# Two chained matrix products on one core: opening with half rows of a, slices of b behind each half

## Chip, cores, metric

One core of a Trainium2 chip. The metric is the device time of the whole kernel in microseconds (us), as the median of several runs. Ratios are the mean time of one kernel's fast runs over that of the kernel before in the same rounds, so they are not quite the ratio of the medians quoted.

## The reference

```python
m, k, n, p = 1024, 1024, 2048, 1024
h = np.matmul(a, b)
h = 0.5 * h * (1 + np.tanh(np.sqrt(2 / np.pi) * (h + 0.044715 * h ** 3)))   # gelu
return np.matmul(h, c).astype(np.float32)
```

## The kernel before

The change touches the first quarter of the kernel. There h11, the first quadrant of h, is made from the first 512 rows of a and the first 1024 columns of b. Block mt of a is 128 rows; slice k of b is 128 rows by 1024 columns (512 KB in float32). Each block is cast to bfloat16 in two halves, each half is turned on TensorE by four 128x128 transposes into PSUM and copied into aT. Each slice is cast and then taken by tiles t (128 columns of b, one PSUM bank each).

```python
for mt in R:                    # R = range(4)
    load_a0(mt, 1)              # whole rows: 128 x 1024 float32, one load
for k in range(KT):             # KT = 8
    load_b0(k, 1)
...
warm_up(8)                      # matmuls without use, that raise the clock
...
for mt in range(3):
    cast_a0(mt, 0)              # left half on VectorE
    cast_a0(mt, 1)              # right half on ScalarE
    pt = [turn0(mt, 0), turn0(mt, 1)]
    ...
    copy0(mt, 0, pt[0])
    copy0(mt, 1, pt[1])
    warm_up((3, 6, 2)[mt])
...
for k in range(1, KT):
    if k + 1 < KT:
        cast_b0(k + 1)
    for t in range(N0 + 1 if k < 4 else N0):    # N0 = 6
        mm0(t, (k,))
```

Later, when the second half of a is turned (the four "turns" on the line of `turn`), tile 6 catches up on four slices and tile 7 on seven. After that nothing differs between the two kernels.

Of the kernel before, what the change touches and what calls it, by code (L numbers as in the profile page):

```python
# [9 lines left out]
F32 = mybir.dt.float32  # L10
BF16 = mybir.dt.bfloat16
# [3 lines left out]
AF = mybir.ActivationFunctionType  # L15
# [4 lines left out]
def kernel(ctx, tc, a, b, c, out):  # L20
    nc = tc.nc
    M, K = a.shape
    _, N = b.shape
    _, P = c.shape
    KT = K // 128
    NT = N // 128
    MT = M // 128
    H = 512
    N0 = 6
    W0 = N // 2  # L30
    KH = KT // 2
    NH = NT // 2
    R = range(4)

    av = a.rearrange("(mt p) k -> p mt k", p=128)
    bv = b.rearrange("(kt p) n -> p kt n", p=128)
# [5 lines left out]
    astage = ctx.enter_context(tc.tile_pool(name="astage", bufs=4))  # L42
    abf = ctx.enter_context(tc.tile_pool(name="abf", bufs=4))
    b0stage = ctx.enter_context(tc.tile_pool(name="b0stage", bufs=6))
    opool = ctx.enter_context(tc.tile_pool(name="opool", bufs=4))
    ppool = ctx.enter_context(tc.tile_pool(name="ppool", bufs=6, space=PSUM))
    tpool = ctx.enter_context(tc.tile_pool(name="tpool", bufs=2, space=PSUM))

    warm = consts.tile([128, H], BF16, name="warm")
# [11 lines left out]
                               for g in range(2)] for h in range(2)]  # L61


    a_st, b_st = {}, {}

    def load_a0(mt, parts):
        st = astage.tile([128, K], F32, name="a_st")
        w = K // parts
        for i in range(parts):
            nc.sync.dma_start(out=st[:, ts(i, w)], in_=av[:, mt, ts(i, w)])  # L70
        a_st[mt] = st

    def load_b0(k, parts):
        st = b0stage.tile([128, W0], F32, name="b0_st")
        w = W0 // parts
        for i in range(parts):
            nc.sync.dma_start(out=st[:, ts(i, w)], in_=bv[:, k, ts(i, w)])
        b_st[k] = st

    gate = consts.tile([128, 1], F32, name="gate")  # L80
    for mt in R:
        load_a0(mt, 1)
    for k in range(KT):
        load_b0(k, 1)

    nc.gpsimd.tensor_copy(gate, b_st[4][:, 0:1])
    g = consts.tile([128, 1], F32, name="g")
    nc.scalar.activation(g, warm[:, 0:1], AF.Gelu_apprx_tanh)

    side = [ppool.tile([128, 8, 128], BF16, name="ps", tag="ps") for _ in range(2)]  # L90
    ps = [ppool.tile([128, H], F32, name="ps", tag="ps") for _ in range(4)]

    def warm_up(n):
        for _ in range(n):
            nc.tensor.matmul(ps[3], warm[:, 0:128], warm, start=True, stop=True)  # L95

    warm_up(8)
    ab = []

    def cast_a0(mt, g):  # L100
        if g == 0:
            ab.append(abf.tile([128, K], BF16, name="ab1"))
            nc.vector.tensor_copy(ab[mt][:, 0:512], a_st[mt][:, 0:512])
        else:
            nc.scalar.activation(ab[mt][:, 512:K], a_st[mt][:, 512:K], AF.Copy)  # L105

    def turn0(mt, g):
        if mt == 2:
            pt = side[g]
        elif (mt, g) == (3, 1):  # L110
            pt = ps[5][:, :].bitcast(BF16).rearrange("p (k m) -> p k m", k=8)
        else:
            pt = tpool.tile([128, 8, 128], BF16, name="pt", tag="pt")
        for k in range(4):
            nc.tensor.transpose(pt[:, k, :], ab[mt][:, ts(4 * g + k, 128)], ident)  # L115
        return pt

    def copy0(mt, g, pt):
        dst = aT[0][:, ts(g, 4), ts(mt, 128)]
        if g == 0 or mt == 3:  # L120
            nc.vector.tensor_copy(dst, pt[:, 0:4, :])  # L121
        else:
            nc.scalar.activation(dst, pt[:, 0:4, :], AF.Copy)  # L123

    HW = W0 // 2

    def cast_b0(k):
        v = {0: ((HW, W0),), 1: ((0, 256), (256, HW))}.get(k, ((0, HW),))
        a = {0: ((0, 256), (256, HW))}.get(k, ((HW, W0),))
        for i in range(max(len(v), len(a))):  # L130
            if i < len(a):
                nc.scalar.activation(b_lo[:, k, slice(*a[i])], b_st[k][:, slice(*a[i])], AF.Copy)  # L132
            if i < len(v):
                nc.vector.tensor_copy(b_lo[:, k, slice(*v[i])], b_st[k][:, slice(*v[i])])  # L134

    for mt in range(3):
        cast_a0(mt, 0)
        cast_a0(mt, 1)
        pt = [turn0(mt, 0), turn0(mt, 1)]
        if mt == 2:  # L140
            cast_a0(3, 0)
        copy0(mt, 0, pt[0])
        copy0(mt, 1, pt[1])
        warm_up((3, 6, 2)[mt])
    copy0(3, 0, turn0(3, 0))
    warm_up(2)
    ps += [ppool.tile([128, H], F32, name="ps", tag="ps") for _ in range(2)]
    cast_b0(0)
    cast_a0(3, 1)

    def mm0(t, ks):
        for k in ks:
            nc.tensor.matmul(ps[t], b_lo[:, k, ts(t, 128)], aT[0][:, k, :],  # L153
                             start=(k == 0), stop=(k == KT - 1))

    late = [tpool.tile([128, H], F32, name="pt", tag="pt") for _ in range(2)]
    ps += late[::-1]
    for t in R:
        mm0(t, (0,))
    copy0(3, 1, turn0(3, 1))  # L160
    for t in (4, 7, 6, 5):
        mm0(t, (0,))
    cast_b0(1)
    for k in range(1, KT):
        if k + 1 < KT:
            cast_b0(k + 1)
        for t in range(N0 + 1 if k < 4 else N0):
            mm0(t, (k,))

    def gelu(dst, src):  # L170
        nc.scalar.activation(dst, src, AF.Gelu_apprx_tanh)  # L171

    def bank(w=H):
        return ppool.tile([128, w], F32, name="ps", tag="ps", padded_shape=[128, H])
# [6 lines left out]
    for j in R:  # L181
        st = abf.tile([128, K], BF16, name="ab1")
# [7 lines left out]
    def turn(j):  # L190
        pt = ppool.tile([128, KT, 128], BF16, name="ps", tag="ps")
        for k in range(KT):
            nc.tensor.transpose(pt[:, k, :], a1[j][:, ts(k, 128)], ident)  # L193
        nc.vector.tensor_copy(aT[1][:, :, ts(j, 128)], pt)
        nc.scalar.activation(a22[:, :, ts(j, 128)], aT[1][:, KH:KT, ts(j, 128)], AF.Copy)
# [12 lines left out]
                             start=(k == 0), stop=(k == KT - 1))  # L208
        gelu(dst, p)

    mm0(6, range(4, KT))
    gelu(h11[:, 6, :], ps[6])
    mm0(7, range(1, 4))
    turn(0)
    turn(1)
    mm0(7, range(4, KT))
    turn(2)
    gelu(h11[:, 7, :], ps[7])
    mm1_half(0, 0)
# [80 lines left out]
    for j in R:  # L300
        p = bank()
        prod(p, KH, whole(bx), whole(aT[0]), j)
        nc.scalar.activation(v2[:, j, :], p, AF.Copy)
    for j in R:
        p = bank()
# [4 lines left out]
    for j in R:  # L310
        p = bank()
# [8 lines left out]
    for j in R:  # L320
        p = bank()
# [10 lines left out]
    for j in R:  # L332
        p = bank()
# [5 lines left out]
    for j in R:  # L339
        p = bank()  # L340
# [24 lines left out]
    for j in R:  # L365
        p = bank()
# [29 lines left out]
    for j in R:  # L396
        p = bank()
# [4 lines left out]
    for j in R:  # L402
        p = bank()
# [5 lines left out]
    for j in R:  # L409
        p = bank()  # L410
# [8 lines left out]
    for j in R:  # L419
        p = bank()  # L420
# [3 lines left out]
    for j in R:  # L424
        p = bank()
        prod(p, NH, halves(s2), whole(c22), j)
        combine(j, 1, p, p5[:, j, :])
    for j in R:
        p = bank()
        prod(p, NH, whole(h22), pairs(t2), j)  # L430
        combine(4 + j, 0, p, u3[j])
    for j in range(3):
        p = bank()
        prod(p, NH, whole(h12), whole(c21), j)
        combine(j, 0, p, p1[:, j, :])
    for q0, w, queue in ((0, 256, nc.sync), (256, 128, nc.scalar), (384, 128, nc.sync)):
        p = bank(w)
# [33 lines left out]
```

## Time and profile before

| | before |
|---|---|
| median, lowest, highest of the first 3 runs | 120.69, 120.44, 120.73 us |
| span of the profiled run | 118.3 us |
| TensorE busy | 113.4 us, 96% |
| first useful matmul | 10.10 us |
| end of the third turn of the second half of a | 25.67 us |
| landing of b slices 0, 1, 4, 7 | 9.54, 11.63, 15.49, 19.31 us |

The landings are when the last of the 16 increments of a load's semaphore is recorded in the trace.

### The profile page before, as it was taken

The numbers are of one execution on the slowest core, as the hardware profiler recorded it, in microseconds if no ns is written. First come the engines' busy times: TensorE is split into PE (matmuls) and PEld (weight loads), VectorE is DVE, ScalarE is ACT, GpSimd is POOL, SyncE is SP. The second block draws the span as 40 slices with busy tenths as digits, with TensorE's granted clock in tenths as the row PEclk, the third lists the DMA queues.
The fourth block names the chain that finished last, engine by engine and source line by source line (L and its number), as shares of the span: only waits on it lengthen the run. The fifth ranks groups of instructions, "written<-read, shape, count | busy, mean of one in ns | idle before, by whom it ended". The sixth has DMA issues, their size and how long they took to land.

```text
span 118.3 us, 1597 instructions
## 1 busy us (share of the span) xinstructions
PE 113.4 (96%) x583; PEld 76.1 (64%) x589; DVE 82.3 (70%) x113; ACT 45.7 (39%) x77; POOL 26.6 (22%) x39
## 2 busy tenths in 40 slices
PE   5999999999999999999999999999999999999990
PEld 2454444589744445888887447888888888886460
DVE  0355422068999908999999999995789992824450
ACT  5366544978342565206469998330000000000000
POOL 2000069752200000095205329000006500000000
PEclk9999999999999999999999999999999999999999
DMA  3999999999999999959999999999997999944434
GB/s 115 385 395 302 421 418 227 188 368 378 212 209 206 207 205 378 350 137 244 255 229 204 190 195 198 180 206 141 151 159 171 245 266 350 342 184 152 177 118 148
DMA packets 13543, 28.41 MB, mean 240 GB/s; under 512 B 992, under 2 KB 5472, under 8 KB 13536
## 3 DMA queue, kind: packets, MB, share of 16 engines
q0 software_dynamic: 9216, 17.83, 73.0%
q1 hardware_dynamic: 4176, 10.42, 23.6%
q8 instruction: 4, 0.07, 0.2%
q10 hardware_dynamic: 144, 0.07, 0.2%
q14 instruction: 3, 0.02, 0.1%
HBM read 20.97 MB, written 4.19 MB: 213 GB/s over the span
## 4 chain that ended last, share of the span: by engine, by line
PE 95%; ACT 1%; DVE 1%; issue 1%
PE ps L269 64%; PE ps L153 9%; PE ps L207 7%; PE ps L95 4%; PE ps L200 4%; PE pt L153 3%; PE ps L193 2%; PE pt L115 1%; PE ps L115 1%; ACT aT L123 1%; ACT ab L105 0%; DVE aT L121 0%; DVE ot L440 0%; DVE warm L50 0%
## 5 line engine op out<-in xcount | busy, mean ns | idle before, releaser
L269 PE MATMUL ps<-t,s 128*128 128x512 f32 x64 | 14.9, 392 | 0.0
L269 PE MATMUL ps<-c,h 128*128 128x512 bf16 (+2 forms) x78 | 14.1, 336 | 0.1
L269 PEld LDWEIGHTS ps<-t,s 128*128 128x128 f32 x64 | 12.0, 188 | 2.6
L277 DVE TENSOR_TENSOR ot<-ps,v 128x512 f32<-128x512 f32 x16 | 10.4, 681 | 3.2 <-PE ps L269 3.2
L269 PE MATMUL ps<-t,h 128*128 128x512 f32 x48 | 11.7, 389 | 0.0
L171 ACT ACTIVATE h<-ot 128x512 bf16<-128x512 f32 (+1 forms) x16 | 9.4, 622 | 5.9 <-DVE ot L277 5.9
L269 PEld LDWEIGHTS <-h 128*128 128x128 bf16 x80 | 7.1, 98 | 7.0 <-issue 0.5
L171 ACT ACTIVATE h<-ps 128x512 bf16<-128x512 f32 (+2 forms) x17 | 8.3, 526 | 8.4 <-PE ps L207 5.9
L153 PE MATMUL ps<-aT,b_lo 128*128 128x512 bf16 x46 | 11.2, 379 | 0.2
L385 DVE TENSOR_TENSOR ot<-ps,p 128x512 f32<-128x512 f32 x11 | 7.5, 688 | 5.5 <-PE ps L269 3.1
L153 PEld LDWEIGHTS <-b_lo 128*128 128x128 bf16 x64 | 6.1, 98 | 7.5 <-DVE b_lo L134 0.5
L269 PEld LDWEIGHTS ps<-t,h 128*128 128x128 f32 x48 | 9.0, 188 | 1.9
L207 PE MATMUL ps<-aT,b_lo 128*128 128x512 bf16 x39 | 8.7, 379 | 0.1
L95 PE MATMUL ps<-warm 128*128 128x512 bf16 x21 | 7.1, 475 | 1.2 <-DVE warm L50 1.2
L269 PE MATMUL ps<-as,bt 128*128 128x512 f32 x32 | 7.6, 396 | 0.0
L287 POOL DMA_DIRECT2D c<-in_c_dram x8 | 6.3, 833 | 5.6 <-DMA b<-in_b_dram 3.9
L269 PE MATMUL ps<-as,b 128*128 128x512 f32 x32 | 7.4, 389 | 0.0
L269 PE MATMUL ps<-c,s 128*128 128x512 f32 x32 | 7.4, 389 | 0.0
L269 PE MATMUL ps<-aT,bx 128*128 128x512 bf16 x31 | 7.0, 379 | 0.1
L418 POOL DMA_DIRECT2D t<-c x4 | 3.5, 1042 | 15.5 <-PE ps L269 14.4
L132 ACT ACTIVATE b_lo<-b_st 128x512 bf16<-128x512 f32 (+1 forms) x9 | 5.1, 581 | 4.8 <-DMA b_st<-in_b_dram 4.8
L134 DVE CAST b_lo<-b_st 128x512 bf16<-128x512 f32 (+1 forms) x9 | 3.5, 394 | 5.0 <-DMA b_st<-in_b_dram 5.0
(71 smaller groups left out, 172.0 us busy)
## 6 DMA issues: line engine op xcount, KB each, us to landing
b_st<-in_b_dram SPq DMA_DIRECT2D x8, 512.0 KB, 8.9
out_dram<-ot SPq DMA_DIRECT2D x15, 256.0 KB, 2.1
c<-in_c_dram POOLq DMA_DIRECT2D x6, 512.0 KB, 17.8
t<-c POOLq DMA_DIRECT2D x6, 512.0 KB, 6.6
a_st<-in_a_dram SPq DMA_DIRECT2D x4, 512.0 KB, 4.8
b<-in_b_dram POOLq DMA_DIRECT2D x2, 1024.0 KB, 10.3
c<-in_c_dram POOLq DMA_DIRECT2D x2, 1024.0 KB, 20.7
t<-t POOLq DMA_DIRECT2D x4, 512.0 KB, 8.6
```

The lines of the kernel that those rows point to most:

```text
L95: nc.tensor.matmul(ps[3], warm[:, 0:128], warm, start=True, stop=True)
L132: nc.scalar.activation(b_lo[:, k, slice(*a[i])], b_st[k][:, slice(*a[i])], AF.Copy)
L134: nc.vector.tensor_copy(b_lo[:, k, slice(*v[i])], b_st[k][:, slice(*v[i])])
L153: nc.tensor.matmul(ps[t], b_lo[:, k, ts(t, 128)], aT[0][:, k, :], start=(k == 0), stop=(k == KT - 1))
L171: nc.scalar.activation(dst, src, AF.Gelu_apprx_tanh)
L200: nc.tensor.matmul(p, b_lo[:, k, ts(t, 128)], aT[1][:, k, ts(q, 256)], start=(k == 0), stop=(k == KT - 1))
L207: nc.tensor.matmul(p, b_lo[:, k, ts(t, 128)], aT[h][:, k, :], start=(k == 0), stop=(k == KT - 1))
L269: nc.tensor.matmul(p, lhs(t)[:, ts(j, 128)], rhs(t)[:, q], start=(t == 0), stop=(t == n - 1))
L277: tt(ot, p, u, op=ADD)
L287: nc.gpsimd.dma_start(out=dst[:, t:t + 4, :], in_=cv[:, r * NH + t:r * NH + t + 4, ts(q, H)])
L385: tt(ot, p, u, op=ADD)
L418: nc.gpsimd.dma_start(out=t2[i], in_=c21[:, P2[i], :], accum_op=ADD)
```

## The change

Its intent is to have useful matmuls sooner. With the left half rows of a alone, four of the eight slices of b can be used. So 1 MB of a comes first, then four slices, then the right half rows, then four slices. Seven tiles take every slice, in place of seven and then six. The turns need PSUM while seven tiles are open: the first turns use banks of tiles that have not begun, the second ones the bank of tile 7, one half of it for even blocks and one for odd.

```diff
-    for mt in R:
-        load_a0(mt, 1)
-    for k in range(KT):
-        load_b0(k, 1)
+    for g in range(2):
+        load_a0(g)               # four loads: 128 x 512 each
+        for k in range(g * KH, g * KH + KH):
+            load_b0(k)
 ... (cut)
+    def turned(mt, g):
+        if g == 0:
+            return ps[mt][:, :].bitcast(BF16)[:, 0:512].rearrange("p (k m) -> p k m", k=4)
+        return ps[7][:, :].bitcast(BF16)[:, ts(mt % 2, 512)].rearrange("p (k m) -> p k m", k=4)
 ... (cut: four left halves are cast, turned and copied, with 10 warm-ups between)
+    for k in range(KH):
+        if k + 1 < KH:
+            cast_b0(k + 1)
+        else:
+            cast_a0(0, 1, True)
+            cast_a0(1, 1, False)
+        for t in range(7):
+            mm0(t, (k,))
+            if k + 1 == KH and t == 3:
+                turn0(0, 1)
+                copy0(0, 1, True)          # True: VectorE, False: ScalarE
+    turn0(1, 1)
+    copy0(1, 1, False)
+    cast_a0(2, 1, True)
+    turn0(2, 1)
+    cast_a0(3, 1, True)
+    copy0(2, 1, False)
+    turn0(3, 1)
+    copy0(3, 1, True)
+    for k in range(KH, KT):
+        cast_b0(k)
+        for t in range(7):
             mm0(t, (k,))
 ... (cut)
-    mm0(6, range(4, KT))
     gelu(h11[:, 6, :], ps[6])
-    mm0(7, range(1, 4))
+    mm0(7, range(KH))
     turn(0)
     turn(1)
-    mm0(7, range(4, KT))
+    mm0(7, range(KH, KT))
```

More of the change, by code (lines that the diff above doesn't have):

```diff
@@ L61, with load_a0, load_b0 @@
                                for g in range(2)] for h in range(2)]
-    a_st, b_st = {}, {}
-    def load_a0(mt, parts):
-        st = astage.tile([128, K], F32, name="a_st")
-        w = K // parts
-        for i in range(parts):
-            nc.sync.dma_start(out=st[:, ts(i, w)], in_=av[:, mt, ts(i, w)])
-        a_st[mt] = st
-    def load_b0(k, parts):
-        st = b0stage.tile([128, W0], F32, name="b0_st")
-        w = W0 // parts
-        for i in range(parts):
-            nc.sync.dma_start(out=st[:, ts(i, w)], in_=bv[:, k, ts(i, w)])
-        b_st[k] = st
+    a_st = [astage.tile([128, K], F32, name="a_st") for _ in R]
+    b_st = {}
+    def load_a0(g):
+        for mt in R:
+            nc.sync.dma_start(out=a_st[mt][:, ts(g, H)], in_=av[:, mt, ts(g, H)])
+    def load_b0(k):
+        b_st[k] = b0stage.tile([128, W0], F32, name="b0_st")
+        nc.sync.dma_start(out=b_st[k], in_=bv[:, k, 0:W0])
     gate = consts.tile([128, 1], F32, name="gate")
-    for mt in R:
-        load_a0(mt, 1)
-    for k in range(KT):
-        load_b0(k, 1)
+    for g in range(2):
+        load_a0(g)
+        for k in range(g * KH, g * KH + KH):
+            load_b0(k)
     nc.gpsimd.tensor_copy(gate, b_st[4][:, 0:1])
@@ L88, with cast_a0, copy0 @@
     nc.scalar.activation(g, warm[:, 0:1], AF.Gelu_apprx_tanh)
-    side = [ppool.tile([128, 8, 128], BF16, name="ps", tag="ps") for _ in range(2)]
-    ps = [ppool.tile([128, H], F32, name="ps", tag="ps") for _ in range(4)]
+    ps = [ppool.tile([128, H], F32, name="ps", tag="ps") for _ in range(N0)]
+    ps += [tpool.tile([128, H], F32, name="pt", tag="pt") for _ in range(2)]
     def warm_up(n):
         for _ in range(n):
-            nc.tensor.matmul(ps[3], warm[:, 0:128], warm, start=True, stop=True)
+            nc.tensor.matmul(ps[5], warm[:, 0:128], warm, start=True, stop=True)
     warm_up(8)
-    ab = []
-    def cast_a0(mt, g):
+    ab = [abf.tile([128, K], BF16, name="ab1") for _ in R]
+    def turned(mt, g):
         if g == 0:
-            ab.append(abf.tile([128, K], BF16, name="ab1"))
-            nc.vector.tensor_copy(ab[mt][:, 0:512], a_st[mt][:, 0:512])
+            return ps[mt][:, :].bitcast(BF16)[:, 0:512].rearrange("p (k m) -> p k m", k=4)
+        return ps[7][:, :].bitcast(BF16)[:, ts(mt % 2, 512)].rearrange("p (k m) -> p k m", k=4)
+    def cast_a0(mt, g, vector):
+        if vector:
+            nc.vector.tensor_copy(ab[mt][:, ts(g, H)], a_st[mt][:, ts(g, H)])
         else:
-            nc.scalar.activation(ab[mt][:, 512:K], a_st[mt][:, 512:K], AF.Copy)
+            nc.scalar.activation(ab[mt][:, ts(g, H)], a_st[mt][:, ts(g, H)], AF.Copy)
     def turn0(mt, g):
-        if mt == 2:
-            pt = side[g]
-        elif (mt, g) == (3, 1):
-            pt = ps[5][:, :].bitcast(BF16).rearrange("p (k m) -> p k m", k=8)
-        else:
-            pt = tpool.tile([128, 8, 128], BF16, name="pt", tag="pt")
+        pt = turned(mt, g)
         for k in range(4):
             nc.tensor.transpose(pt[:, k, :], ab[mt][:, ts(4 * g + k, 128)], ident)
-        return pt
-    def copy0(mt, g, pt):
+    def copy0(mt, g, vector):
         dst = aT[0][:, ts(g, 4), ts(mt, 128)]
-        if g == 0 or mt == 3:
-            nc.vector.tensor_copy(dst, pt[:, 0:4, :])
+        if vector:
+            nc.vector.tensor_copy(dst, turned(mt, g))
         else:
-            nc.scalar.activation(dst, pt[:, 0:4, :], AF.Copy)
+            nc.scalar.activation(dst, turned(mt, g), AF.Copy)
     HW = W0 // 2
@@ L134, in cast_b0 @@
                 nc.vector.tensor_copy(b_lo[:, k, slice(*v[i])], b_st[k][:, slice(*v[i])])
-    for mt in range(3):
-        cast_a0(mt, 0)
-        cast_a0(mt, 1)
-        pt = [turn0(mt, 0), turn0(mt, 1)]
-        if mt == 2:
-            cast_a0(3, 0)
-        copy0(mt, 0, pt[0])
-        copy0(mt, 1, pt[1])
-        warm_up((3, 6, 2)[mt])
-    copy0(3, 0, turn0(3, 0))
-    warm_up(2)
-    ps += [ppool.tile([128, H], F32, name="ps", tag="ps") for _ in range(2)]
+    cast_a0(0, 0, True)
+    turn0(0, 0)
+    warm_up(2)
+    cast_a0(1, 0, False)
+    copy0(0, 0, True)
+    turn0(1, 0)
+    warm_up(2)
+    cast_a0(2, 0, True)
+    copy0(1, 0, False)
+    turn0(2, 0)
+    warm_up(2)
+    cast_a0(3, 0, True)
+    copy0(2, 0, False)
+    turn0(3, 0)
+    warm_up(4)
+    copy0(3, 0, True)
     cast_b0(0)
-    cast_a0(3, 1)
     def mm0(t, ks):
@@ L154, in mm0 @@
                              start=(k == 0), stop=(k == KT - 1))
-    late = [tpool.tile([128, H], F32, name="pt", tag="pt") for _ in range(2)]
-    ps += late[::-1]
-    for t in R:
-        mm0(t, (0,))
-    copy0(3, 1, turn0(3, 1))
-    for t in (4, 7, 6, 5):
-        mm0(t, (0,))
-    cast_b0(1)
-    for k in range(1, KT):
-        if k + 1 < KT:
-            cast_b0(k + 1)
-        for t in range(N0 + 1 if k < 4 else N0):
+    for k in range(KH):
+        if k + 1 < KH:
+            cast_b0(k + 1)
+        else:
[17 more added lines that the diff above has]
+        for t in range(7):
             mm0(t, (k,))
```

## The prediction

> **What bounds the kernel now.** I read the page first (busy rows, then the chain that ended last), then the chain in order of time, then the timeline and one-microsecond windows of the first 31 us, where the whole change lies.
>
> The page's busy rows and chain:
>
> ```profile
> PE 113.4 (96%) x583; PEld 76.1 (64%) x589; DVE 82.3 (70%) x113; ACT 45.7 (39%) x77; POOL 26.6 (22%) x39
> ...
> PE 95%; ACT 1%; DVE 1%; issue 1%
> ```
>
> TensorE is on the chain for 95% of 118.3 us. So the time is what TensorE has to do, plus the start before it has useful work, plus its gaps. The chain in order of time (start, length, what) has almost no gaps after 12 us:
>
> ```profile
> 1.19 3.59 PE ps L95 x8
> 4.79 0.81 PE pt L115 x8
> ...
> 9.63 0.44 DVE aT L121
> 10.06 0.04 issue
> 10.10 0.38 PE ps L153
> ...
> 20.71 1.24 PE ps L153 x5
> 21.95 1.51 PE pt L153 x7
> 23.47 0.89 PE ps L193 x16
> 24.36 0.86 PE pt L153 x4
> 25.22 0.45 PE ps L193 x8
> 25.67 0.87 PE ps L200 x8
> ```
>
> The reader should see two things. The first useful matmul (L153) starts at 10.10; everything before is warm-up and turning of a. From then on matmuls of 128x512 follow each other at 1.51/7 = 0.216 us, up to the third turn of the second half of a, which ends at 25.67. I use that end as the yardstick: what follows (L200, L207, L269) is not touched and TensorE runs it without a wait of its own, with pieces of "issue" of at most 0.05 us. A shift of the yardstick should reach the end one for one.
>
> The inputs arrive meanwhile. From the timeline of ACT (start, length, what, idle before):
>
> ```profile
> 4.17 0.63 ACT L105 ACTIVATE ab<-a_st 128x512 bf16<-128x512 f32 x1 [1.93 <-DMA a_st<-in_a_dram]
> 11.66 0.63 ACT L132 ACTIVATE b_lo<-b_st 128x512 bf16<-128x512 f32 x1 [0.85 <-DMA b_st<-in_b_dram]
> 15.52 0.63 ACT L132 ACTIVATE b_lo<-b_st 128x512 bf16<-128x512 f32 x1 [0.65 <-DMA b_st<-in_b_dram]
> 19.34 0.63 ACT L132 ACTIVATE b_lo<-b_st 128x512 bf16<-128x512 f32 x1 [0.63 <-DMA b_st<-in_b_dram]
> ```
>
> The first block of a lands at 4.17, b slice 1 at 11.66, slice 4 at 15.52, slice 7 at 19.34: 1.28 us for a slice of 512 KB. Six tiles take 6 x 0.216 = 1.29 us, so TensorE keeps pace with the slices, just behind them. The windows (PE, PEld, DVE, ACT, POOL busy, clock, DMA share, GB/s) show the queue as full:
>
> ```profile
> 6.00:7.00 1.00, 0.72 (x10) 0.44 (x9) 0.49 (x2) 0.74 (x2) 0.00 (x0) 1.00 1.00 406
> 10.00:11.00 1.00, 0.86 (x5) 0.49 (x6) 0.38 (x2) 0.81 (x2) 0.00 (x0) 1.00 0.96 274
> 13.00:14.00 1.00, 1.00 (x6) 0.43 (x5) 0.37 (x1) 0.57 (x1) 0.00 (x0) 1.00 1.03 422
> 26.00:27.00 1.00, 1.00 (x15) 0.94 (x14) 0.40 (x1) 0.57 (x2) 0.29 (x1) 1.00 1.25 406
> ```
>
> About 400 GB/s except for a dip from 8 to 11 us, and the clock is granted in full.
>
> **What the Trainium skill says.**
> "PSUM — Partial Sum Buffer", section "PSUM bank collisions raise a hardware error": two engines must not touch one bank and quadrant at once, even in different columns; "Semaphore-guard PSUM by bank × quadrant (by bank is the simple version), not by address." In the kernel before no two turns in a row share a bank, so its trace neither confirms nor denies it. It is the point on which my number rests.
> "TensorE: Matmul & The Clock Gate", Part 1, "The HAM clock gate": the clock falls to half after an idle window of about 3.4 us. The trace agrees as to the start: 8 warm-ups take 3.59 us, 0.45 each, later ones 0.22. No gap before is long enough to test the fall.
> "DMA: Bandwidth & Descriptors", "Specifications": line rate needs at least 512 bytes a run. Half rows of a are 2,048 bytes. The trace agrees: the loads of b12 and b22 also have 2,048-byte runs and move 406 GB/s at 26 us. I expect no loss from splitting rows.
> "ScalarE: Activation LUTs", "What ACT_TABLE_LOAD costs": 186 ns + 0.833 per element, 612 ns for 512; the trace has 0.60 to 0.63.
>
> **The change part by part.**
> 1. Order of loads. Before: 2 MB of a, then 4 MB of b. After: 1 MB of a, 2 MB of b, 1 MB of a, 2 MB of b. The sum is the same and the queue is the bound, so slice 7 still lands near 19.3 and slice 4 near 15.5 (all of a and five slices precede it in both). Slice 0 moves forward by 1 MB: it has 1.57 MB in front of and in it; the windows' rates add up to that by 6.1 us, and the landings above lag the added rates by about 0.8 us: 6.9 us, or 7.5 if the dip comes with it.
> 2. First useful matmul. The eight cold warm-ups still hold TensorE to 4.79. Then come four turns of four transposes, ten warm-ups, and four copies. With 0.43 us from the start of a turn to its copy (9.20 to 9.63 in the trace), 0.42 for a copy on VectorE and 0.60 on ScalarE, and the casts (0.43, 0.62) early enough: copies at 5.3, 6.05, 6.7 and 7.4, the last ends 7.8; VectorE casts its half of slice 0 by 8.25; the warm-ups end near 8.1. First useful matmul 8.15 instead of 10.10. Gain 1.95 us.
> 3. Work now behind the first useful matmul that lay before it: 12 transposes more than the four of the kernel before, 12 x 0.055 = 0.66 us. Loss 0.66 us. The sum of useful matmuls of this stage is 64 in both.
> 4. The four slices. Seven tiles are 7 x 0.2155 = 1.51 us per slice, slower than a slice arrives, so TensorE does not wait: slice 3 starts at 8.15 + 21 x 0.2155 = 12.68, and its fourth tile ends at 13.54, where the first turn of the second half-row stands. That part of a landed near 12.5 and is cast by 13.0.
> 5. The hole. All four second turns go to tile 7's bank. If the bank is guarded as a whole, turn and copy alternate: with VectorE copying 0.43 + 0.42 + 0.05 = 0.90, with ScalarE 0.44 + 0.60 + 0.05 = 1.09. So turns at 13.54, 14.44, 15.53, 16.62; the last copy (VectorE) ends at 17.47. Slice 4 landed at 15.5, but VectorE's queue has its cast behind that copy: 17.90, and the next matmul at 17.95. From 13.54 to 17.95 are 4.41 us, of which TensorE has three matmuls (0.65) and 16 transposes (0.89): a hole of 2.87 us. The matmuls before the change have about 0.15 us of such hole after 10.10 (at slice 0). Loss 2.7 us.
> 6. After it. Slices 5 to 7 have all landed in time (19.34 against a need at 22.5), so 28 matmuls run in 6.03 us, to 23.98. Then 4 for tile 7 (0.86), 16 transposes (0.89), 4 (0.86), 8 transposes (0.45): 27.04. The loads of the other half of a that these turns need are still released by slice 4 at 15.5 and landed by 25.6 before; the third turn is at 26.6, so they are not waited for.
>
> Sum: -1.95 + 0.66 + 2.7 = +1.4 us; the same from the yardstick, 27.04 - 25.67 = +1.37.
>
> **The rivals.**
> A. The two halves of tile 7's bank are guarded by address. Then the third turn waits only for the first's copy and its own cast, the fourth for the second's copy: third 14.9, its copy on ScalarE behind the second one, fourth 15.55, last copy ends 16.4, cast of slice 4 by 16.8, next matmul 16.9. The hole shrinks by about 1.05 us: +0.35 us in all. For it: the halves alternate, which looks like the intent. Against it: the skill's rule. I give it one in four.
> B. The gain wins: only if the hole closes down to the landing of slice 4 and its cast (15.95). Then the yardstick ends near 25.05: -0.6 us. Against it: VectorE and ScalarE are strict queues and the cast of slice 4 stands behind the copies. One in twelve.
> C. The clock falls in the hole. For it: 4.41 us with TensorE one third busy. Against: no idle piece over about 1 us, and the skill asks for an idle window. If it falls, some 16 matmuls cost 0.21 more: 3.4 us, +4.8 in all at worst, +3 if only part of a window. One in nine.
> D. Slice 0 or 1 lands late because the dip (274 GB/s at 10 us, when the first slices moved) travels with b. It costs up to 0.6 us at the start of the matmuls, and is mostly hidden behind the copies, which end at 7.8 anyway.
>
> **Range and chances.** The main path gives 120.69 + 1.4 = 122.1. Weighed with A and B below it and C and D above it, I put the time at 121.9. Eight in ten: from 120.6 (between A and B) to 123.3 (the main path with half of C or all of D). 2% is 2.4 us. Faster by over 2% has no mechanism, since at best 0.6 us can be won: 0.01. Slower by over 2% needs C, or D together with longer steps: 0.14. Within 2%: 0.85.
>
> **What would show it.** Step 1: slice 4 landing near 15.5 and slice 7 near 19.3. Step 2: the first L153-type matmul near 8.15. Step 5: the four copies out of tile 7's bank one after another with no transposes running beside them, and TensorE idle in pieces between 14.4 and 17.95, waiting on aT copies and then on VectorE's cast of b_lo. Step 6: the third turn of the later half ending near 27.0. Rival A shows as a turn that starts while the copy of the other half runs; C as matmuls of the fifth slice spaced by 0.43 and a clock row under 9 near 18 us. The number would be wrong if TensorE began to wait somewhere after 27 us, or if the later stages took up the delay: then the span would move by less than the yardstick.

## More of the kernel before

Besides the lines that the prediction shows, two windows of the kernel before will be compared later. The columns are the window, its length, the busy time and count of each engine (PE, PEld, DVE, ACT, POOL), the granted clock, the DMA share and GB/s.

```profile
3.00:6.00 3.00, 3.00 (x16) 1.29 (x14) 1.13 (x3) 1.01 (x2) 0.00 (x0) 1.00 1.01 389
6.00:9.00 3.00, 2.72 (x26) 1.61 (x25) 1.59 (x5) 1.89 (x5) 0.00 (x0) 1.00 0.99 385
```

The reader is to see the last number: 389 and 385 GB/s while a and the first slice come in.

## The result, and the profile after

The changed kernel takes 123.66 us (median of 6 runs, 123.17 to 125.07) against 120.56 (6 runs, 120.31 to 121.0): a ratio of 1.0258, with a 95% interval of 1.0205 to 1.031. The prediction said 121.9 and at most 123.3, so the loss was foreseen and its size was not.

The page of the changed kernel, busy row of the engines and chain by engine:

```profile
PE 113.6 (93%) x586; PEld 75.7 (62%) x586; DVE 82.7 (68%) x114; ACT 45.1 (37%) x76; POOL 26.3 (22%) x39
...
PE 87%; DMA 6%; ACT 1%; SPq 1%; DVE 1%; issue 0%
```

TensorE does the same work (113.6 us against 113.4), but a transfer is now on the chain with 6%. The chain in order of time (start, length, what) says which:

```profile
2.59 7.06 DMA b_st<-in_b_dram
...
10.15 1.47 PE ps L149 x6
...
15.72 0.22 PE pt L109 x4
...
16.59 0.27 PE pt L109 x4
...
16.88 0.61 ACT aT L116
...
17.53 0.40 PE pt L109 x4
...
17.95 0.60 ACT aT L116
...
19.09 0.42 DVE aT L114
19.52 0.41 DVE b_lo L127
...
19.97 1.47 PE ps L149 x6
...
28.81 0.45 PE ps L199 x8
```

Two things are to be read. First, the load of slice 0 was issued at 2.59 and has landed only at 9.66, although 1 MB less stands ahead of it than before (9.54 there). The first useful matmul is at 10.15, where it was 10.10 before: the change has won no time there. Second, from the first turn of the right halves (15.72 in the chain; 15.56 by the start of its record) turn and copy alternate, and the next matmul is at 19.97. That is the hole, 4.41 us from record to record (the fourth turn is not in the chain; it stands in the timeline further down).

The third turn of the later half ends at 28.81 + 0.45 = 29.26, against 25.67: 3.6 us later. From there to the last VectorE instruction of the chain it is 89.9 us in both kernels. The spans of the profiled runs differ by 3.9 us; the last 0.3 lies after that instruction. Those two runs took 123.94 and 120.05, so the profiled run of the changed kernel is on the upper side of its six.

The same windows as before:

```profile
3.00:6.00 3.00, 2.90 (x16) 1.27 (x15) 0.85 (x2) 0.63 (x1) 0.00 (x0) 1.00 0.95 302
6.00:9.00 3.00, 2.54 (x17) 0.87 (x14) 1.28 (x3) 1.19 (x2) 0.00 (x0) 1.00 0.94 247
```

302 and 247 GB/s in place of 389 and 385. The bytes moved do not tell the whole: the 16 increments of slice 0 come from 6.82 to 9.66 us, where before they lay within 0.6. Some of the parts of the transfer were done at the time that the prediction gave, and the last one 2.8 us later. Slice 7 lands at 21.56 in place of 19.31, with its increments still 2.3 us apart.

### The profile page after: what moved, and what is told of

Its sections match the earlier page's. It is cut to its first block, busy times and chain, and to the rows that moved or that the text cites. A ratio compares the mean times of both kernels' runs of the same rounds, so it can differ in the third digit from the quotient of the medians.

```text
span 122.2 us, 1602 instructions
## 1 busy us (share of the span) xinstructions
PE 113.6 (93%) x586; PEld 75.7 (62%) x586; DVE 82.7 (68%) x114; ACT 45.1 (37%) x76; POOL 26.3 (22%) x39
## 4 chain that ended last, share of the span: by engine, by line
PE 87%; DMA 6%; ACT 1%; SPq 1%; DVE 1%; issue 0%
PE ps L274 62%; PE ps L149 9%; PE ps L213 7%; DMA b_st<-in_b_dram 6%; PE ps L206 4%; PE pt L149 3%; PE ps L199 1%; SPq L69 1%; ACT aT L116 1%; PE pt L109 1%; DVE b_lo L127 1%; ACT b_lo L125 0%; DVE aT L114 0%; DVE ot L445 0%
## 5 line engine op out<-in xcount | busy, mean ns | idle before, releaser
L149 PE MATMUL ps<-aT,b_lo 128*128 128x512 bf16 x48 | 11.8, 379 | 2.3 <-DVE b_lo L127 2.3
L213 PE MATMUL ps<-aT,b_lo 128*128 128x512 bf16 x40 | 8.8, 379 | 0.0
L89 PE MATMUL ps<-warm 128*128 128x512 bf16 x18 | 6.4, 491 | 1.2 <-DVE warm L50 1.2
L200 DVE COPY aT<-ps 128x1024 bf16<-128x1024 bf16 x4 | 2.7, 689 | 6.6 <-PE ps L199 6.6
L274 PEld LDWEIGHTS ps<-as,bt 128*128 128x128 f32 x32 | 6.0, 188 | 1.4
```

The source lines that it names most:

```text
L89: nc.tensor.matmul(ps[5], warm[:, 0:128], warm, start=True, stop=True)
L149: nc.tensor.matmul(ps[t], b_lo[:, k, ts(t, 128)], aT[0][:, k, :], start=(k == 0), stop=(k == KT - 1))
L200: nc.vector.tensor_copy(aT[1][:, :, ts(j, 128)], pt)
L213: nc.tensor.matmul(p, b_lo[:, k, ts(t, 128)], aT[h][:, k, :], start=(k == 0), stop=(k == KT - 1))
L274: nc.tensor.matmul(p, lhs(t)[:, ts(j, 128)], rhs(t)[:, q], start=(t == 0), stop=(t == n - 1))
```

## The experiments

Three questions were open: what makes slice 0 late, whether the hole is the shared bank, and whether the clock plays a part. All kernels below gave the right result. Where a profiled run was slow, its times are not compared. The ratios of e2, e3, e6, e8 and e9 have intervals that overlap the changed kernel's own (1.0205 to 1.031), and they come from other batches; a difference of 1 us or less from the changed kernel is therefore only as good as the trace beside it.

### Loads alone, in the kernel before

**e1_rowwise**: two half-row loads in place of one, in the old order.

```diff
-        load_a0(mt, 1)
+        load_a0(mt, 2)
```

> The kernel before, only each row block of a comes in two half-row parts, one right after the other; order of the data unchanged. Theory S (splitting rows in half makes the early loads slow and uneven): slice 0 of b lands 1 us or more later than the 9.5 us of before, and the kernel is 1 us or more slower. Theory D (the first slices of b are slow whatever stands ahead of them, and moving them forward moved the slow stretch with them): within 0.3 us of before. Theory P (only reading the same half of all rows in a run is slow): within 0.3 us too.

Measured: ratio 1.012 (1.007 to 1.017), 1.4 us slower; slice 0 at 11.72 (9.54 before), slice 7 at 20.65 (19.31). By the time, splitting alone does harm, clear of the noise though under 2%, and theories D and P, which said no more than 0.3 us, fall. The windows:

```profile
3.00:6.00 3.00, 3.00 (x15) 1.60 (x14) 1.18 (x3) 0.96 (x2) 0.00 (x0) 1.00 0.87 233
6.00:9.00 3.00, 1.30 (x13) 0.73 (x12) 0.86 (x3) 1.00 (x3) 0.00 (x0) 1.00 0.96 270
```

**e1_colwise**: four left halves, four right halves, then b.

```diff
-    for mt in R:
-        load_a0(mt, 1)
+    for g in range(2):
+        for mt in R:
+            nc.sync.dma_start(out=a_st[mt][:, ts(g, H)], in_=av[:, mt, ts(g, H)])
```

> The kernel before, only a comes as four left half-row parts and then four right ones, then b. Theories S and P: slower by 1 us or more, first useful matmul after 11 us. Theory D: within 0.5 us of before, except that the casts of the right halves of the first blocks come up to 3 us later and may hold up the turns a little.

Measured: ratio 1.039 (1.0316 to 1.0463). It is slower, as S and P said, but by far more than the loads explain: the right halves come late, TensorE stood nearly idle from 6 to 8.6 us, and the warm-ups behind that took 0.43 us again. The clock confounds it, so it separates nothing beyond what the row-wise split shows.

**e4_partition_split**: eight loads again, but of 64 partitions with whole rows.

```diff
-            nc.sync.dma_start(out=st[:, ts(i, w)], in_=av[:, mt, ts(i, w)])
+            nc.sync.dma_start(out=st[ts(i, 64), :], in_=av[ts(i, 64), mt, :])
```

> The kernel before, each block of a in two loads of 64 partitions with whole rows of 4 KB: eight loads of a, runs as long as before. Theory R (runs of 2 KB are what slows the early loads): like before, within 0.4 us of it, slice 7 of b near 19.3. Theory N (the larger number of smaller loads slows them): like the row-wise split, 1.4 us slower than before, slice 7 near 20.6.

Measured: ratio 1.0305, and neither theory's number: the loads of a moved 242, 227 and 223 GB/s from 3 to 12 us, evenly, and slice 7 landed at 22.73. The experiment was badly chosen. The Trainium skill says so beforehand ("SBUF — State Buffer", section "Door 1: The DMA port swizzle"): partitions 0 to 63 reach only 8 of the 16 ports, 196 GB/s at 1 MiB. The trace agrees in kind, with 223 to 242. It tells nothing of the question.

**e5_pair_loads_before**: four loads, each the half rows of two blocks. The runs stay 2,048 bytes; only the number of loads goes back to four. (The staging buffers become two of twice the size; the later users of that memory share them in the same order.)

```diff
-    for mt in R:
-        load_a0(mt, 1)
+    for i in range(2):
+        st = astage.tile([128, 2, K], F32, name="a_st")
+        for g in range(2):
+            nc.sync.dma_start(out=st[:, :, ts(g, H)], in_=av[:, 2 * i:2 * i + 2, ts(g, H)])
```

> The kernel before, a in four loads, each the half rows of two blocks: runs of 2 KB, no more loads than before. Theory R: slices land late as in the row-wise split (slice 7 near 20.6), 1.4 us slower. Theory N: slice 7 near 19.3 to 19.6; the time within 0.6 us of before (the right half of block 0 comes 1.3 us later than before, which may cost the turns a little).

Measured: slice 7 at 19.70, near theory N's 19.3 to 19.6 and well short of R's 20.6. The time missed both: ratio 1.0148, 1.8 us slower, and its four runs were 121.67 (the profiled one) and three near 122.8. In the trace the first useful matmul is at 11.75: the right half of block 0 is cast only at 6.10, and the last block of a lands at 9.47 (8.27 before). So the loss here sits in the turns, not in the last slices. The rates in the two windows, 341 and 354 GB/s, stand between those of the kernel before and of the row-wise split. Slice 0 landed at 10.75. With one trace each, 9.54, 10.75 and 11.72 do not yet separate the theories; the trace of e2 below says why.

### Loads alone, in the changed kernel

**e2_old_loads**: the changed kernel with whole rows of a first and then b.

```diff
-    for g in range(2):
-        load_a0(g)
-        for k in range(g * KH, g * KH + KH):
-            load_b0(k)
+    for mt in R:
+        nc.sync.dma_start(out=a_st[mt], in_=av[:, mt, :])
+    for k in range(KT):
+        load_b0(k)
```

> The changed kernel with the loads of before (whole rows of a, then b). If what the change lost beyond the hole is only the late slice 0 (9.66 us in the changed kernel, 9.5 in the kernel before), the first useful matmul is again near 10.1, the hole behind the fourth slice is again 4.4 us from first turn to next matmul, and the time is within 0.5 us of the changed kernel (123.7). If the interleaved loads themselves cost later on (slice 7 at 21.6 against 19.3), it is over 0.5 us faster than the changed kernel.

Measured: ratio 1.0339 (1.0282 to 1.0396), some 0.9 us slower than the changed kernel, where both branches had it within 0.5 us or faster. So the new order of the loads is worth something, about 0.9 us by these ratios (at full clock 124.25 and 124.26 against 123.31 and 123.38), even with its uneven landing; the loss lies in the rest of the plan. Its profiled run was slow, but one thing in it bears on the loads. They are those of the kernel before, whole rows of 512 KB, yet slice 0 landed at 10.65 (9.54 there) and slice 7 at 20.41 (19.31), with the parts of slice 0 1.35 us apart. So landings can differ by about 1 us with loads of the same size and order, and the 9.54 of the kernel before is one trace.

**e6_pair_loads_after** and **e8_pair_warm**: half rows of two blocks in one load; in e8 also three more warm-ups.

```diff
-        for mt in R:
-            nc.sync.dma_start(out=a_st[mt][:, ts(g, H)], in_=av[:, mt, ts(g, H)])
+        for i in range(2):
+            nc.sync.dma_start(out=a_two[i][:, :, ts(g, H)], in_=av[:, 2 * i:2 * i + 2, ts(g, H)])
 ... (e8 only)
-    warm_up(8)
+    warm_up(11)
```

> The changed kernel with the half rows of two blocks in one load: four loads of a in place of eight. Theory N: slice 0 lands near 7.5 in place of 9.7, first useful matmul near 8.5, and the kernel is 1.0 to 1.6 us faster than the changed one (122.2). Theory R: within 0.5 us of the changed kernel (123.7).

Measured for e6: ratio 1.0204 (1.0124 to 1.0284), some 0.65 us faster than the changed kernel, which is within the noise; theory N had asked for 1.0 at least. The profiled run was slow, so it was repeated with more warm-ups:

> The changed kernel with the half rows of two blocks in one load, as before, and 11 warm-ups ahead of the first turn in place of 8, so that TensorE does not stand idle from 4.8 to 5.6 us, after which the earlier run with paired loads showed its matmuls at 0.43 us until 10 us. If the late first useful matmul there (10.7 with slice 0 landed at 7.6) came from the low clock alone: warm-ups at 0.22 from about 5.5 us, first useful matmul at 8.4 to 9.0, time near 122.0. If it came from the later landing of the first pair (5.1 against 3.4): first useful matmul still after 10, time near 123.4.

Measured for e8: ratio 1.0204 (1.0146 to 1.0262). Slice 0 lands at 7.62 and slice 7 at 20.02. The first useful matmul is at 9.26, between the two expectations: the first pair is there only at 4.86, and the eleven warm-ups ran until 6.06 at 0.44 us each, since the clock had not risen. Two of its runs at full clock took 122.56 and 122.70, two at 0.982 and 0.984 of it 123.78 and 124.13.

**e11_changed_again**: the changed kernel once more, no edit, for a second trace.

> The changed kernel once more, for a second trace. If the uneven landing is a property of its loads: slice 0 is cast after 9 us again, and slice 7 lands after 20.5 us. If it was an accident of the first trace: slice 0 near 7.5, slice 7 near 19.5 and a span near 120.5.

Measured: slice 0 at 9.19, slice 7 at 21.68. It was no accident. Together with the runs below, the changed order was traced four times with eight loads of 256 KB (the changed kernel, its repeat, e3, e9) and twice in the fast state with four of 512 KB (e8, e10). Slice 0 landed at 9.66, 9.19, 9.24 and 8.97 with eight, and at 7.62 and 7.43 with four; slice 7 at 21.56, 21.68, 21.44 and 21.46 against 20.02 and 19.91. The slow runs of e6 and e7, with four, have 7.64 and 7.89, and 19.82 and 20.06. Bytes, order and length of the runs are the same, and the two groups lie further apart than the traces within each. So cutting the loads of a into 256 KB in place of 512 is what makes slice 0 1.4 to 2.2 us late. What happens inside the transfer engines that sets them apart is not shown. Four loads are also issued sooner (slice 0 at 1.73 us in place of 2.59); that this plays no part was not tested, though the engines were 95% busy from 3 to 6 us with eight. Packets of 2 KB alone are not it: the paired loads have them too, and in the trace of the changed kernel they take 84 ns as a rule where 4 KB take 159, 6% more per byte.

### The hole

**e3_pair_copies**: the right halves of two blocks are turned into tile 7's bank together, and one copy of 1,024 columns empties it.

```diff
-            if k + 1 == KH and t == 3:
-                turn0(0, 1)
-                copy0(0, 1, True)
-    turn0(1, 1)
-    copy0(1, 1, False)
-    ... (two more of each)
+            if k + 1 == KH and t == 3:
+                turn_pair(0)               # eight transposes, one copy on VectorE
+    cast_a0(2, 1, True)
+    cast_a0(3, 1, False)
+    turn_pair(2)
```

> The changed kernel with the second turns in pairs: eight transposes fill tile 7's bank, one copy empties it, twice. Theory B (the bank is the hole): turn, copy, turn, copy takes about 3.1 us from the first turn to the next matmul in place of 4.41, 1.3 us less, and the kernel is 1.2 us faster than the changed one (about 122.4). Theory L (the hole is really the late landing of slice 4, at 17.8 in the changed kernel): no more than 0.3 us faster.

Measured: ratio 1.0168 (1.0117 to 1.0219), 0.9% or 1.1 us better than the changed kernel's, close to the 1.2 of theory B. Slice 4 landed at 17.65, hardly sooner than the 17.78 there. From its chain:

```profile
17.27 0.63 PE pt L109 x8
...
19.01 1.47 PE ps L149 x6
```

The next matmul comes at 19.01, 3.6 us after the first turn at 15.37; of that, 0.34 is a wait for the cast of block 2 that I had not counted. Fewer copies shorten the hole as well, so this run does not single out the bank; the next one does.

**e9_two_banks**: tile 6 joins tile 7 in taking its slices at the end, so that even and odd blocks have a bank each.

```diff
-        return ps[7][:, :].bitcast(BF16)[:, ts(mt % 2, 512)]...
+        return ps[6 + mt % 2][:, :].bitcast(BF16)[:, 0:512]...
-        for t in range(7):          # in both loops over k
+        for t in range(6):
 ...
+    mm0(6, range(KT))
     gelu(h11[:, 6, :], ps[6])
```

> The changed kernel, but tile 6 takes no slice until the end, as tile 7, so that the second turns use two banks in turn. Theory B (one bank holds turn and copy apart): turns run beside copies, and from the first turn to the next matmul about 3.1 us in place of 4.41, the rest limited by slice 4 (17.8); after that six tiles a slice wait for slice 7 (21.6), so the gain is about 1.0 us: 122.7. If the bank does not matter: no turn starts during a copy, and the time is within 0.4 us of the changed kernel.

Measured: ratio 1.0185 (1.0137 to 1.0233), 0.9 us better than the changed kernel's. The timeline (start, length, what, idle before it and what ended that):

```profile
16.22 1.16 ACT L116 ACTIVATE aT<-pt 128x512 bf16<-128x512 bf16 x2 [0.49 <-PE pt L109]
...
16.34 0.40 PE L109 MATMUL pt<-ident,ab 128*128 128x128 bf16 x4 [0.16 <-DVE ab L102]
...
18.25 1.47 PE L149 MATMUL ps<-aT,b_lo 128*128 128x512 bf16 x6 [0.95 <-DVE b_lo L127]
```

A turn starts at 16.34 while ScalarE is copying the one before it (from 16.22), which never happens in the changed kernel. From its timeline, the third and the fourth turn:

```profile
17.53 0.38 PE L109 MATMUL pt<-ident,ab 128*128 128x128 bf16 x4 [0.69 <-ACT aT L116]
...
18.59 0.38 PE L109 MATMUL pt<-ident,ab 128*128 128x128 bf16 x4 [0.69 <-ACT aT L116]
```

Both wait for a copy on ScalarE (16.88 to 17.48 and 17.95 to 18.55), and the second turn, at 16.46, follows VectorE's copy (15.98 to 16.40): every turn follows the copy of the turn before it, though that copy empties the other half of the bank. With two banks, 3.15 us pass from the first turn (15.10) to the next matmul, where one bank took 4.41; 0.22 of the difference is the matmul of tile 6 that no longer stands there. So it is the shared bank. The wait is for a semaphore, set by the program; what the hardware would do without it no run shows.

### The clock

The repeat e11 shows something else behind the hole. Two windows from it, each of 2 us:

```profile
20.00:22.00 2.00, 1.92 (x7) 0.82 (x8) 1.08 (x4) 0.93 (x2) 2.00 (x4) 0.74 1.07 207
22.00:24.00 2.00, 2.00 (x6) 0.67 (x5) 0.13 (x1) 0.34 (x1) 2.00 (x4) 0.50 1.10 156
```

The granted clock is 0.74 and then 0.50: six matmuls in the second window where 2 us hold nine. It took 125.75 us (one run, state unknown, so its time is not compared). In the trace the clock is granted by half from 20.98 to 24.39 us. The slow profiled runs of e2 and e6, which have the same hole, show the same: half from 20.83 to 24.24 and from 19.82 to 23.23. This is rival C of the prediction, and it comes in some executions only: the first trace of the changed kernel has the hole and keeps the clock. Of the six runs of the changed kernel, four at 0.995 or more of the full clock took 123.17 to 123.94, and two at 0.986 and 0.983 took 124.67 and 125.07. The first of those two counts among the fast runs; without it their mean is 123.45 in place of 123.69. So the clock explains about 0.2 us of the 3.1. Of the runs of the kernel before in the three batches of experiments, none had less than 0.997.

### All mends together

**e7_pairs_all** and **e10_pairs_all_warm**: paired loads, paired turns, and the cast of slice 4 ahead of the last copy; e10 has 11 warm-ups too.

```diff
     cast_a0(3, 1, False)
+    cast_b0(KH)
     turn_pair(2)
```

> The same, with the second turns in pairs (eight transposes, one copy) and the cast of slice 4 ahead of the last copy. The hole should shrink by 1.0 us as in the run with paired copies and by up to 0.4 more. Theory N: 120.5 to 121.0, level with the kernel before. Theory R: near 122.4.

Measured for e7: two fast runs of 121.24 and 120.86, ratio 1.0024 (0.9986 to 1.0062); two of 123.17, which the rule sets apart although their clock is recorded as 1.0, and the profiled one is among them. Its trace has no clock entry before 10.62 us; until then the warm-ups take 0.43 us each, and the first useful matmul comes at 11.19. So it was run again, with more warm-ups:

> All mends together: loads in pairs, second turns in pairs with one copy each, the cast of slice 4 ahead of the last copy, 11 warm-ups. If the late start, the hole and the clock are all of the loss, it is level with the kernel before or a little faster: 119.9 to 120.8. If something else of the change costs time too: 121.5 or more.

Measured for e10: six fast runs, 121.01 to 121.57, ratio 1.0034 (0.9996 to 1.0071). That is level with the kernel before and 2.2% better than the changed kernel, though not the lead that the expectation allowed. Windows and chain of e10:

```profile
3.00:6.00 3.00, 3.00 (x10) 1.07 (x9) 0.43 (x1) 0.63 (x1) 0.00 (x0) 1.00 1.00 381
6.00:9.00 3.00, 3.00 (x26) 1.85 (x25) 1.33 (x4) 1.49 (x4) 0.00 (x0) 1.00 0.91 296
```

```profile
9.59 1.29 PE ps L150 x6
...
17.95 1.46 PE ps L150 x6
```

The rate is back at 381 in the first window; the 296 in the second is the slow stretch that the traces here (e4's apart) have somewhere before 11 us. First useful matmul 9.59, next matmul behind the hole 17.95 against 19.97. No version that I found beats both kernels.

## Why the prediction was wrong

Its working stands by steps; the figures are of the profiled run. Step 1 failed, and with it the gain of step 2; the costs that were set against the gain came within 0.2 us of the prediction.

1. **Order of loads (step 1): failed.** "Slice 0 moves forward by 1 MB ... 6.9 us, or 7.5 if the dip comes with it", and slice 7 "still lands near 19.3". Measured: 9.66 and 21.56. The wrong premise stands in the part on the skill: "I expect no loss from splitting rows". I had checked the length of the runs against a later stage, which moves 1 MB loads, and took the rate over; I had not asked what loads of half the size do. With loads of 512 KB in the same order, slice 0 landed at 7.43 and 7.62: the arithmetic of the step was sound, its loads were not.
2. **First useful matmul (step 2): the term that was mis-sized.** A gain of 1.95 us was put in; measured 10.15 against 10.10, a loss of 0.05. That is 2.0 of the 2.2 us by which the yardstick ended later than predicted (29.26 against 27.04). The other 0.2 is the fill of the pipeline at a first matmul, left out of the sum (six matmuls in 1.47 against 1.29). A second part of the step was off and stayed hidden: the last copy ended at 8.44, not 7.8, since the third and fourth loads of a landed only at 6.20 and 7.07 and their casts came after that. With slice 0 in time the step would have given about 8.9 (an estimate: 8.44, a cast of 0.43 and 0.05), a gain of 1.2 and not 1.95.
3. **Transposes moved behind the first matmul (0.66): not measured apart.** The timeline shows them where the prediction put them.
4. **The hole (step 5): right.** From first turn to next matmul 4.41 predicted, 4.41 measured. It is not luck: from turn to turn 0.90, 1.09 and 1.09 were predicted and 0.90, 1.07 and 1.06 measured, and it was the shared bank, as two banks show. Slice 4 landed at 17.78, later than the 15.5 of step 1, but VectorE's cast of it was still behind the last copy, at 19.52, so that did not lengthen the hole.
5. **After it (step 6): right**, all later by the same amount; slice 7 at 21.56 was still early for a need at 24.5.
6. **Rivals.** A fell: no turn ran beside a copy. B did not come. C came in some runs, and its argument against it ("no idle piece over about 1 us") failed. D named the right place, a late slice 0, but put it at 0.6 us and hid it behind the copies. The upper end of the range was also added up too low: the main path, 122.1, with half of C's 3.4 us is 123.8, not 123.3.

The sum with the measured first term, and the terms for transposes and hole as predicted, is +0.05 + 0.66 + 2.7 + 0.2 = +3.6 us, the 3.6 by which the yardstick moved. The last three are measured together: from the first useful matmul to the yardstick are 19.11 us, 15.57 before, 3.54 more. The medians differ by 3.1, since the profiled run was one of the slower.

So the direction was right: the hole costs more than the earlier start could have won. The size was wrong, because the earlier start did not come.

## What to carry to other kernels

Before counting on data "1 MB sooner", ask whether the loads keep their size: here, cutting 512 KB loads into 256 KB ones took back the whole lead, and one load over two tiles' worth brought slice 0 to 7.4 to 7.6 us. The first useful matmul gained less by it (9.26 and 9.59 in place of 10.15), because the first pair came later and the warm-ups then held TensorE. Two halves of one PSUM bank were not two buffers here: turn and copy alternated, so empty a bank by one copy, or use two banks. And behind a stretch in which TensorE was only a quarter busy (0.78 of 3.2 us in the repeat) the clock fell in some executions, though no single idle piece was over 1.1 us.

## What the Trainium skill lacked or had wrong

- "DMA: Bandwidth & Descriptors", "Specifications", gives a least run for line rate (512 bytes), which runs of 2,048 meet. Its section "Rules for kernel authors" does ask for 1 MiB or more per load for the highest rate, which the prediction did not weigh; the 512 KB loads of the kernel before moved 389 and 385 GB/s all the same. No page that I read says what several loads of 256 KB in a full queue do to one another: here 302 and 247 GB/s in place of 389 and 385, the parts of one load landing 2.8 us apart in place of 0.6, and not back in step even at slice 7 (2.3 us apart).
- "TensorE: Matmul & The Clock Gate", Part 1, speaks of an idle window of about 3.4 us before the clock falls; its passage "A second HAM failure mode" adds that frequent short idle pieces can make the clock swing as well, which the prediction's argument against C passed over. What is lacking is how little work is too little. In the repeat of the changed kernel the clock fell to 0.50 at 20.98, after 3.2 us (16.9 to 20.1) in which eight transposes ran, TensorE was busy for 0.78 us and no idle piece was over 1.1 us; in the first trace the like stretch (0.77 of 3.12 us) left it at 1.00.
- No page tells of the slow stretch at the start: in the traces here, e4's apart, the loads lose speed for 2 to 6 us somewhere before 11 us (the kernel before: 274 GB/s from 10 to 11 us, 422 from 13 to 14), in another place when the loads are cut otherwise.
